# The order of VectorE and ScalarE written by hand through the mixers of a hybrid decoder step, with two open decay levels, sample values loaded ahead of states and the third gates moved up

## The chip, the core and the metric

The kernel runs on one core of one Trainium2 chip. The metric is the device time in microseconds (us) of one execution on that core, the median of several runs. The engines are TensorE (PE, its weight loads PEld), VectorE (DVE), ScalarE (ACT), GpSimd (POOL) and SyncE (SP); in this kernel SyncE issues the DMAs of the weights, and GpSimd those of the samples' states and values.

## The reference, cut

One layer of a decoder with 256 prompt tokens and 8 samples of one new token each (NP = 256, NT = 264 columns of work). The weights are float32.

```python
h = rmsnorm(x, g_pre_mix) * (1.0 + sc1) + sh1       # sc1, sh1, ... = silu(c) @ w_ada: "ada"
z = h @ w_in
(z_uv, hq, hf, hi, hg, gq, gk, gv, gr, glr, z_gate) = split(z)

y_a = spatial_gating(u, layernorm(v), sgu_w_s, sgu_b_s)                # branch A
o_hg, S_hg = gated_linear_recurrence(q_hg, k_hg, hi, log_f, s_hg)      # HGRN, 8 heads
y_b = head_rmsnorm(o_hg, hg_norm_g) * silu(hg)                         # branch B
o_g, S_g = gated_linear_recurrence(q_g, k_g, gv, log_a, s_gla)         # GLA, 4 heads
y_c = head_rmsnorm(o_g, gla_norm_g) * silu(gr)                         # branch C
merged = sum(sigmoid(z_gate)[n] * (branches[n] @ w_branch[n]) for n in range(3))
x = x + gt1 * rmsnorm(merged @ w_out, g_post_mix)
x = x + gt2 * rmsnorm(square(relu(h2 @ w_mlp_up)) @ w_mlp_down, g_post_mlp)
```

A recurrence is `S = f * S + k v^T; o = S^T q` per token. For the prompt it starts from zero; each sample has a state of its own, read from memory, changed by its one token and written back.

## The kernel before, in words

**Granules.** All large products run as a chain of granules of 512 KB of weights, 24 matmuls each: a weight tile is split into a rounded half `whi` (a cast on ScalarE, L109) and the remainder `wlo` (a subtraction on VectorE, L106), and TensorE forms hi x hi, hi x lo and lo x hi (L602 to L604) into an accumulator `mm`. `plan()` lists the granules in order, and SyncE loads them five ahead into four `raw` buffers. The split halves live in six buffers, two to a granule (`SPLIT_AHEAD = 2`), so what is written behind granule p for VectorE or ScalarE stands in program order behind the split of granule p+3.

In order of time the granules are: the input products (0 to 79), the GLA inputs (80 to 113), branch A (114 to 161), the four gate tiles of branch B, `gates_b` (162 to 177), branch B (178 to 225), `gates_c` (226 to 241), branch C (242 to 289), then `w_out` and the MLP, 577 in all. A branch tile is a gate product of four granules and two granules of the branch's own weights; L1296 (branch A) or L1298 with an addition of L103 (B and C) multiplies the two.

**Background.** The mixers run between granules. Generators `mixer_a` (spatial gating), `mixer_r` (one each for HGRN heads 0 to 3 and 4 to 7, and for GLA: groups 0, 1, 2) and `samples_r` (the samples' states of each group) are moved on by `background()` after every granule, at a rate from `RATES`; `READY` stands for the next granule. `mixer_r` forms the gates (`log_sigmoid`, L925 to L931, for group 0 with `lower_bounds`, L906 to L920, ahead, then L961 to L973), opens decay levels whose matmuls (L633) wait in the list `levels`, and ends with the attention between the two halves of 128 tokens: the key product `kd` and the query product `qd` (L1163, L1165, and L100 of VectorE), eight matmuls at L1176, a copy `attx`. `slot()` issues waiting level matmuls and sample reads between granules; the ada products (L342) fill in too.

**Samples.** For each step, `samples_r` loads a state `st` of 256 KB (`fetch`, L1029) and values `vbc` (`values`, L1035), both from GpSimd's queue; ScalarE scales the state (L1055), VectorE adds key times value (L1057), GpSimd stores it (L1058), and when a sample's heads are complete its state is read by L640 into `sm` and added to `os`. At the end stand a square with its sum (L1067), the root by small VectorE instructions (`rstd_small`, L179 to L185) and a scaling (L1069). `FETCHED` is the number of granules between a load and its use. `finish(i)`, at the head of branches B and C, drains what is left of group i, transposes `os` on TensorE (L1256) and copies it (L1257); `parts_c` then multiplies by the gates (L1335) and splits the result for TensorE.

**Who sets the order.** From the first mixer to the last branch (L898 to the exit behind branch 2) TensorE and GpSimd follow the program as written (`manual_schedule`); VectorE's and ScalarE's instructions are placed by the compiler's scheduler.

Of the kernel before, what the change touches and what calls it, by code (L numbers as in the profile page):

```python
# [15 lines left out]
P = 128  # L16
# [31 lines left out]
READY = object()  # L48
SLOT_WAIT = 4
HELD_OWED = 1.0  # L50
LEVELS_HELD = 3
FETCHED = 3
AGE = 2
ADA_LAND = 4

# [2 lines left out]
def hybrid_step_kernel(  # L58
# [438 lines left out]
    rate = [0.0, 0.0]  # L497
# [8 lines left out]
    def plan():  # L506
# [9 lines left out]
        for s in range(4):  # L516
            out += blocks(win, 0, KT, 7168 + s * CW)
        for n in range(N_BRANCH):
            if n:
                g0 = 5120 if n == 1 else 8192  # L520
                for s in range(4):
                    out += blocks(win, 0, KT, g0 + s * CW)
            for m in range(8):
                out += blocks(win, 0, KT, 9232 + n * D + m * CW) + blocks(w_branch[0, n], 0, 8, m * CW)
# [285 lines left out]
    def mixer_a():  # L810
# [71 lines left out]
        for gp in range(4):  # L882
# [12 lines left out]
            )  # L895
            mul(u[:, :, 0:NP], yv[:, :, 0:NP], u[:, :, 0:NP])
            yield
    order = tc.manual_schedule(engines={mybir.EngineType.PE, mybir.EngineType.Pool})  # L898
    order.__enter__()
    gen_a = mixer_a()  # L900
    bg.g.append(gen_a)
# [112 lines left out]
    def samples_r(G):  # L1014
# [12 lines left out]
        def fetch(b, h):  # L1027
            st = tmp([P, nh, dv], "st", ST_BUFS)
            nc.gpsimd.dma_start(st, G.s_in(b, h, nh))  # L1029
            ahead.append((st, now[0]))  # L1030

        def values(b, h):
            v = tmp([P, 4, P], "vbc", VB_BUFS)
            r0 = 4 * nj * b + h * nj
            nc.gpsimd.dma_start(v, vs_d[G.i, r0:r0 + 4, :].partition_broadcast(P))  # L1035
            vals.append((v.rearrange("p (h j) v -> p h (j v)", h=nh), now[0]))
# [8 lines left out]
        for n, (b, h0) in enumerate(steps):  # L1045
            if n + 2 < len(steps):

                yield lambda: len(sts) + sum(len(x[3]) for x in samples) <= ST_BUFS - 3
                fetch(*steps[n + 2])
            if n + 1 < len(steps):  # L1050
                values(*steps[n + 1])
            yield lambda: now[0] >= max(ahead[0][1] + FETCHED, vals[0][1] + FETCHED - 1)
            st, v = ahead.pop(0)[0], vals.pop(0)[0]
            for i in range(nh):
# [18 lines left out]
    def mixer_r(G):  # L1073
# [83 lines left out]
            levels.append((now[0], e, e, m, put))  # L1157

        cv = v4(c, P)
        yield lambda: len(levels) < 2  # L1160
        kd, qd = blk([P, 4, NP]), blk([P, 4, P])
        sub(kd.rearrange("p h (n j) -> p h n j", j=P), cv[:, :, :, 127:128].to_broadcast([P, 4, 2, P]), cv)
        S.activation(qd, c[:, :, P:NP], AF.Exp)  # L1163
# [6 lines left out]
        mul(kd, kd, k[:, :, 0:NP])  # L1170
        yield READY
        yield READY
        attx = blk([P, 4, P])
        ps = sm([P, 4, P])
        for h in range(4):
            T.matmul(ps[:, h, :], kd[:, h, 0:P], qd[:, h, :], start=True, stop=True)  # L1176
# [167 lines left out]
    branch(0, parts_a)  # L1344
    gates_b = gate_tiles(5120)
    rounds.batch = 2
    branch(1, lambda: parts_b(gates_b))
    rate[:] = RATES[2]
    rounds.pace, rounds.batch = 4, 4
    gates_c = gate_tiles(8192)  # L1350
    rate[:] = RATES[3]
    branch(2, lambda: parts_c(gates_c))

    order.__exit__(None, None, None)
# [367 lines left out]
```

## Time and profile before

| what | value |
|---|---|
| median of 3 runs (lowest, highest) | 1940.76 us (1939.07, 1942.31) |
| span of the profiled execution | 1942.9 us (2.1 over that median) |
| TensorE busy / weight loads | 98% / 93% |
| VectorE, ScalarE, GpSimd busy | 61%, 52%, 4% |
| mean granted TensorE clock | 0.994 |
| DMA moved | 442.06 MB, 228 GB/s on the mean |

How to read it. The profile is one execution, and its span runs from the first to the last instruction. TensorE's busy share is the first thing to see: nothing else is near it. A wait is quoted as engine, operation and line, the releaser with its line, then total us, count, longest. A row of a busy-time stretch gives `start:end length`, then busy us and instruction counts of PE, PEld, DVE, ACT and POOL, then the granted clock (1.00 is full), the busy share of the DMA engines and GB/s. In grouped rows `x8` is a count and `busy, mean ns` follow; time in brackets is idle time ahead of an instruction with its releaser. Numbers at the end of tile names (`sm_1835_11308`) are buffer numbers.

### The profile page before, as it was taken

Reading aid. Unit: us, or ns where it says so; the run is one execution under the profiler, and the core shown is the slowest. Engines: PE = TensorE matmul, PEld = TensorE weight load, DVE = VectorE, ACT = ScalarE, POOL = GpSimd, SP = SyncE. Lnnn points to the kernel's source line nnn. Section 1 sums busy time; section 2 is a strip of 40 time slices with the busy share of each in tenths; the row PEclk is TensorE's granted clock in tenths of the full one; section 3 lists DMA queues with packets and bytes.
Section 4 is the critical chain, followed back from the end, with each engine's and each line's share of the span. In section 5 each row is a group of like instructions: output and inputs, shape, how many; then the busy total and the mean of one; then the engine's idle time right before and its main releaser. Section 6 shows DMA issues by size and latency. Waiting matters only on the chain.

```text
span 1942.9 us, 42324 instructions
## 1 busy us (share of the span) xinstructions
PE 1903.4 (98%) x17080; PEld 1812.1 (93%) x17080; DVE 1186.1 (61%) x2103; ACT 1006.5 (52%) x1825; POOL 83.9 (4%) x142
## 2 busy tenths in 40 slices
PE   6999999998999999999999999999999999999998
PEld 5989999988999998999999988999999999999997
DVE  4566667686578695565555666545556555555665
ACT  5444454665666765544444556444444545454444
POOL 1000000001001112200000010000000000000000
PEclk9999999999999999999999999999999999999999
DMA  9897786688588688987777846776566555555552
GB/s 317 299 337 247 249 287 213 214 250 276 175 262 290 214 258 283 306 266 249 253 256 233 300 129 195 229 226 199 178 182 184 179 180 184 177 183 182 179 183 99
DMA packets 339380, 442.06 MB, mean 228 GB/s; under 512 B 14930, under 2 KB 281024, under 8 KB 339184
## 3 DMA queue, kind: packets, MB, share of 16 engines
q1 hardware_dynamic: 329120, 409.62, 65.5%
q0 software_dynamic: 8992, 28.48, 4.6%
q8 instruction: 134, 2.20, 0.5%
q10 hardware_dynamic: 1072, 1.25, 0.2%
q14 instruction: 62, 0.51, 0.1%
HBM read 427.60 MB, written 11.70 MB: 226 GB/s over the span
## 4 chain that ended last, share of the span: by engine, by line
PE 95%; DMA 2%; issue 1%; ACT 1%; DVE 1%; POOL 0%; SPq 0%; ACTq 0%; DVEq 0%; POOLq 0%
PE mm L602 29%; PE mm L603 29%; PE mm L604 28%; PE ada L342 3%; PE ada L274 1%; PE sm L633 1%; PE sm L780 1%; DMA raw<-in_w_in_dram 1%; PE sm L640 0%; DMA b<-in_x_prompt_dram 0%; DMA vbc<-vs_d 0%; DVE wlo L106 0%; DMA b<-in_w_ada_dram 0%; ACT gt L1515 0%; PE sm L1176 0%
## 5 line engine op out<-in xcount | busy, mean ns | idle before, releaser
L602 PE MATMUL mm<-b,whi 128*128 128x264 f32 x4624 | 1326.6, 287 | 7.5 <-ACT b L109 3.5
L603 PE MATMUL mm<-b,whi 128*128 128x264 f32 x4624 | 1317.8, 285 | 0.8 <-DVE b L106 0.8
L604 PE MATMUL mm<-b,wlo 128*128 128x264 f32 x4624 | 1314.5, 284 | 1.4 <-issue 0.7
L106 DVE TENSOR_TENSOR wlo<-raw,whi 128x512 fp32r<-128x512 f32 x1136 | 775.5, 689 | 572.0 <-ACT whi L109 570.0
L109 ACT CAST whi<-raw 128x512 fp32r<-128x512 f32 x1136 | 695.4, 618 | 730.6 <-PE mm L603 654.5
L602 PEld LDWEIGHTS mm<-b,whi 128*128 128x128 f32 x4624 | 872.3, 189 | 49.1 <-issue 26.2
L604 PEld LDWEIGHTS mm<-b,wlo 128*128 128x128 f32 x4624 | 872.5, 189 | 2.2 <-DVE wlo L106 1.1
L603 PEld LDWEIGHTS mm<-b,whi 128*128 128x128 f32 x4624 | 872.2, 189 | 1.4 <-DVE b L106 1.3
L103 DVE TENSOR_TENSOR b<-b,mm 128x528 f32<-128x528 f32 (+1 forms) x137 | 95.7, 700 | 42.7 <-PE mm L604 42.7
L1057 DVE SCALAR_TENSOR_TENSOR st<-vbc,b,st 128x128 f32<-128x128 f32 (+1 forms) x96 | 34.1, 389 | 51.1 <-DMA vbc<-vs_d 44.2
L1055 ACT ACTIVATE st<-st,fs 128x128 f32<-128x128 f32 (+1 forms) x96 | 37.0, 430 | 53.0 <-DMA st<-in_state_hgrn_dram 27.0
L274 PE MATMUL ada<-b,cT 128*32 128x256 f32 (+1 forms) x640 | 35.7, 361 | 7.2 <-DMA b<-in_w_ada_dram 7.0
L342 PE MATMUL ada<-araw,cT 128*32 128x512 f32 x296 | 39.9, 601 | 0.0
L274 PEld LDWEIGHTS ada<-b,cT 128*32 128x32 f32 x640 | 18.2, 115 | 19.7 <-issue 6.4
L100 DVE TENSOR_TENSOR b<-b,b 128x512 f32<-128x512 f32 (+1 forms) x47 | 34.1, 740 | 1.4 <-ACT b L1165 0.9
L1058 POOL DMA_DIRECT2D out_dram<-st x32 | 23.5, 735 | 156.6 <-DVE st L1057 150.8
L342 PE MATMUL ada<-b,cT 128*32 128x512 f32 x216 | 26.2, 593 | 0.0
L106 DVE TENSOR_TENSOR b<-gt,b 128x528 fp32r<-128x528 f32 x32 | 22.7, 708 | 3.9 <-ACT whi L109 0.9
L106 DVE TENSOR_TENSOR b<-b 128x1024 f32<-128x1024 f32 (+1 forms) x24 | 24.3, 1016 | 0.0
L109 ACT CAST whi<-araw 128x512 fp32r<-128x512 f32 x20 | 12.4, 621 | 20.7 <-PE mm L603 19.0
L100 DVE TENSOR_TENSOR gt<-vt 128x528 f32<-128x528 f32 x32 | 22.4, 701 | 0.9 <-ACT vt L1581 0.9
L1587 ACT ACTIVATE b<-vt 128x528 fp32r<-128x528 f32 x32 | 20.7, 647 | 1.0
(339 smaller groups left out, 825.2 us busy)
## 6 DMA issues: line engine op xcount, KB each, us to landing
raw<-in_w_in_dram SPq DMA_DIRECT2D x232, 512.0 KB, 4.7
raw<-in_w_mlp_up_dram SPq DMA_DIRECT2D x128, 512.0 KB, 3.7
raw<-in_w_mlp_down_dram SPq DMA_DIRECT2D x128, 512.0 KB, 3.6
b<-in_w_ada_dram SPq DMA_DIRECT2D x102, 512.0 KB, 6.4
araw<-in_w_ada_dram SPq DMA_DIRECT2D x74, 512.0 KB, 6.0
raw<-in_w_branch_dram SPq DMA_DIRECT2D x48, 512.0 KB, 4.5
raw<-in_w_out_dram SPq DMA_DIRECT2D x32, 512.0 KB, 3.9
b<-in_w_ada_dram SPq DMA_DIRECT2D x32, 256.0 KB, 5.7
```

The source lines that it names most:

```text
L100: V.tensor_tensor(o, a, b, op=ALU.mult)
L103: V.tensor_tensor(o, a, b, op=ALU.add)
L106: V.tensor_tensor(o, a, b, op=ALU.subtract)
L109: S.copy(hi, src)
L274: T.matmul(acc[32 * j:32 * j + 32, 0:n], cT[:, k, :], w[:, n * j:n * j + n], start=k == 0, stop=k == KT - 1)
L342: T.matmul(self.acc[32 * j:32 * j + 32, :], cT[:, k, :], ws[j // 2][:, j % 2 * 512:j % 2 * 512 + 512], start=k == 0, stop=k == KT - 1)
L602: T.matmul(o, a, xh(k + j), start=first and j == 0, stop=False)
L603: T.matmul(o, a, xl(k + j), start=False, stop=False)
L604: T.matmul(o, b, xh(k + j), start=False, stop=last and j == n - 1)
L1055: S.activation(st[:, i, :], st[:, i, :], AF.Copy, scale=fs[:, h0 + i, b:b + 1])
L1057: V.scalar_tensor_tensor(st[:, i, :], v[:, i, :], k[:, h0 + i, NP + b:NP + b + 1], st[:, i, :], ALU.mult, ALU.add)
L1058: nc.gpsimd.dma_start(G.s_out(b, h0, nh), st)
```

## The change

It is one edit to who sets the order, and several to what is written in which place.

- VectorE and ScalarE join TensorE and GpSimd in the written order from L898 on.
- `LEVELS_HELD` goes from 3 to 2, and the last stages of a mixer begin when no level is open (`not levels`) instead of when fewer than two are.
- `FETCHED` goes from 3 to 4, and `samples_r` issues `values` ahead of `fetch`, so ahead of the wait of a state load for its buffer.
- `attx` is written into `qd` instead of a new block.
- The granules of `gates_c` move from behind branch B to right behind `gates_b`: granules 178 to 193, and branch B becomes 194 to 241. The rate 1.25 (`RATES[2]`) isn't used any more: the gates run at 1.6, and 1.0 with `pace` and `batch` of 4 is set ahead of branch C.

```diff
--- before.py
+++ after.py
@@ -48,8 +48,8 @@
 READY = object()
 SLOT_WAIT = 4
 HELD_OWED = 1.0
-LEVELS_HELD = 3
-FETCHED = 3
+LEVELS_HELD = 2
+FETCHED = 4
 AGE = 2
 ADA_LAND = 4
 
@@ -516,8 +516,7 @@
         for s in range(4):
             out += blocks(win, 0, KT, 7168 + s * CW)
         for n in range(N_BRANCH):
-            if n:
-                g0 = 5120 if n == 1 else 8192
+            for g0 in (5120, 8192) if n == 1 else ():
                 for s in range(4):
                     out += blocks(win, 0, KT, g0 + s * CW)
             for m in range(8):
@@ -895,7 +894,7 @@
             )
             mul(u[:, :, 0:NP], yv[:, :, 0:NP], u[:, :, 0:NP])
             yield
-    order = tc.manual_schedule(engines={mybir.EngineType.PE, mybir.EngineType.Pool})
+    order = tc.manual_schedule(engines={mybir.EngineType.PE, mybir.EngineType.Pool, mybir.EngineType.DVE, mybir.EngineType.Activation})
     order.__enter__()
     gen_a = mixer_a()
     bg.g.append(gen_a)
@@ -1046,9 +1045,10 @@
             if n + 2 < len(steps):
 
                 yield lambda: len(sts) + sum(len(x[3]) for x in samples) <= ST_BUFS - 3
-                fetch(*steps[n + 2])
             if n + 1 < len(steps):
                 values(*steps[n + 1])
+            if n + 2 < len(steps):
+                fetch(*steps[n + 2])
             yield lambda: now[0] >= max(ahead[0][1] + FETCHED, vals[0][1] + FETCHED - 1)
             st, v = ahead.pop(0)[0], vals.pop(0)[0]
             for i in range(nh):
@@ -1157,7 +1157,7 @@
             levels.append((now[0], e, e, m, put))
 
         cv = v4(c, P)
-        yield lambda: len(levels) < 2
+        yield lambda: not levels
         kd, qd = blk([P, 4, NP]), blk([P, 4, P])
         sub(kd.rearrange("p h (n j) -> p h n j", j=P), cv[:, :, :, 127:128].to_broadcast([P, 4, 2, P]), cv)
         S.activation(qd, c[:, :, P:NP], AF.Exp)
@@ -1170,7 +1170,7 @@
         mul(kd, kd, k[:, :, 0:NP])
         yield READY
         yield READY
-        attx = blk([P, 4, P])
+        attx = qd
         ps = sm([P, 4, P])
         for h in range(4):
             T.matmul(ps[:, h, :], kd[:, h, 0:P], qd[:, h, :], start=True, stop=True)
@@ -1344,11 +1344,10 @@
     branch(0, parts_a)
     gates_b = gate_tiles(5120)
     rounds.batch = 2
+    gates_c = gate_tiles(8192)
     branch(1, lambda: parts_b(gates_b))
-    rate[:] = RATES[2]
+    rate[:] = RATES[3]
     rounds.pace, rounds.batch = 4, 4
-    gates_c = gate_tiles(8192)
-    rate[:] = RATES[3]
     branch(2, lambda: parts_c(gates_c))
 
     order.__exit__(None, None, None)
```

What this moves is seen in three places. (Lines of the changed kernel between about L520 and L1048 have numbers lower by one: its L601 to L603 are L602 to L604 of before, L639 is L640.) A bare row gives line, operation and `out<-in`; `x4` is four instructions.

**VectorE, the end of HGRN group 0**, where `qd` is multiplied (L100, 128x512) for the matmuls of L1176. Before:

```order
L1057 SCALAR_TENSOR_TENSOR st_981_5855<-vbc_1021_6099,b_838_4812,st_981_5855 128x128 x3
L106 TENSOR_TENSOR wlo_1015_6083<-raw_997_5937,whi_1014_6082 128x512
L1057 SCALAR_TENSOR_TENSOR st_981_5855<-vbc_1021_6099,b_838_4812,st_981_5855 128x128
L1057 SCALAR_TENSOR_TENSOR st_1020_6097<-vbc_1022_6110,b_838_4812,st_1020_6097 128x128 x2
L106 TENSOR_TENSOR wlo_1026_6141<-raw_1002_5982,whi_1025_6140 128x512
L1057 SCALAR_TENSOR_TENSOR st_1020_6097<-vbc_1022_6110,b_838_4812,st_1020_6097 128x128
L1296 SCALAR_TENSOR_TENSOR b_985_5863<-gt_1010_6051,mm_1011_6053 128x528
L106 TENSOR_TENSOR wlo_1028_6145<-raw_1002_5982,whi_1027_6144 128x512
L1057 SCALAR_TENSOR_TENSOR st_1020_6097<-vbc_1022_6110,b_838_4812,st_1020_6097 128x128
L106 TENSOR_TENSOR wlo_1032_6177<-raw_1007_6016,whi_1031_6176 128x512
L100 TENSOR_TENSOR b_1018_6089<-b_1018_6089,b_25_170 128x512
L106 TENSOR_TENSOR wlo_1034_6181<-raw_1007_6016,whi_1033_6180 128x512
```

The product stands behind eight sample updates of L1057, in the same granule as the matmuls that read it. After:

```order
L106 TENSOR_TENSOR wlo_1040_6268<-raw_1025_6134,whi_1039_6267 128x512
L106 TENSOR_TENSOR wlo_1042_6272<-raw_1025_6134,whi_1041_6271 128x512
L106 TENSOR_TENSOR b_1044_6277<-b_27_172 128x1024
L100 TENSOR_TENSOR b_1045_6278<-b_1045_6278,b_25_170 128x512
L100 TENSOR_TENSOR b_1044_6277<-b_1044_6277,b_838_4812 128x1024
L1057 SCALAR_TENSOR_TENSOR st_1017_6085<-vbc_1018_6096,b_838_4812,st_1017_6085 128x128 x4
L106 TENSOR_TENSOR wlo_1048_6320<-raw_1031_6170,whi_1047_6319 128x512
L106 TENSOR_TENSOR wlo_1050_6324<-raw_1031_6170,whi_1049_6323 128x512
L103 TENSOR_TENSOR os0_913_5294<-os0_913_5294,sm_1052_6329 128x128
L106 TENSOR_TENSOR wlo_1058_6371<-raw_1036_6204,whi_1057_6370 128x512
L106 TENSOR_TENSOR wlo_1060_6375<-raw_1036_6204,whi_1059_6374 128x512
```

The product stands ahead of the updates of the second of these states (`st_1020` above is `st_1017` here), and L1176 follows two granules later in TensorE's order.

**TensorE, the last sample reads of GLA (L640) and the transposes of their sum (L1256), at the head of branch C.** Before, in two places, fifteen granules apart:

```order
L604 MATMUL mm_1829_11273<-b_49_302,wlo_1810_11178 128x264
L640 MATMUL sm_1835_11308<-st_1784_11015,b_1474_9011 32x256 x2
L640 MATMUL sm_1835_11308<-st_1786_11024,b_1474_9011 32x256 x2
L602 MATMUL mm_1829_11273<-b_231_1274,whi_1814_11215 128x264
```

```order
L604 MATMUL mm_1906_11749<-b_503_2888,wlo_1910_11779 128x264
L1256 MATMUL sm_1929_11892<-cst_83,os2_1518_9296 128x128
L1256 MATMUL sm_1930_11895<-cst_83,os2_1518_9296 128x128
L602 MATMUL mm_1935_11914<-b_49_302,whi_1912_11808 128x264
```

In the first the states of the last sample are read between the first and the second granule of `gates_c`, and in the second the transposes stand between the last granule of `gates_c` and the first of branch C. After:

```order
L602 MATMUL mm_1906_11785<-b_1551_9569,whi_1894_11720 128x264
L603 MATMUL mm_1906_11785<-b_1550_9568,wlo_1895_11721 128x264
L639 MATMUL sm_1917_11861<-st_1870_11565,b_1511_9285 32x256 x2
L639 MATMUL sm_1917_11861<-st_1872_11574,b_1511_9285 32x256 x2
L1256 MATMUL sm_1923_11885<-cst_83,os2_1559_9609 128x128
L1256 MATMUL sm_1924_11888<-cst_83,os2_1559_9609 128x128
L601 MATMUL mm_1929_11907<-b_49_302,whi_1897_11755 128x264
```

The reads have moved to the transposes, with nothing between them; all stand between the last granule of branch B and the first of branch C. On VectorE the chain between them reads in the changed kernel:

```order
L106 TENSOR_TENSOR wlo_1913_11850<-raw_1896_11724,whi_1912_11849 128x512
L106 TENSOR_TENSOR wlo_1915_11854<-raw_1896_11724,whi_1914_11853 128x512
L1298 SCALAR_TENSOR_TENSOR gt_1905_11783<-gt_1905_11783,mm_1906_11785 128x528
L103 TENSOR_TENSOR b_1258_7581<-b_1258_7581,gt_1905_11783 128x528
L103 TENSOR_TENSOR os2_1559_9609<-os2_1559_9609,sm_1917_11861 128x256
L179 TENSOR_SCALAR sx_1921_11871<-sss_1918_11867 128x1
L181 TENSOR_SCALAR srr_1919_11868<-sx_1921_11871 128x1
L100 TENSOR_TENSOR sa_1922_11872<-srr_1919_11868 128x1
```

The sum `os2` and the root behind it stand after the two operations on branch B's last tile (L1298 and L103), which wait for that last granule; eight more small rows of the root follow.

**ScalarE, the gates of HGRN group 0.** Before:

```order
L925 ACTIVATE b_819_4695<-b_27_172 128x1056
L109 CAST whi_803_4627<-raw_782_4492 128x512
L927 ACT_TABLE_LOAD
L927 ACTIVATE b_819_4695<-b_819_4695 128x1056
L109 CAST whi_805_4631<-raw_782_4492 128x512
L109 CAST whi_808_4662<-raw_789_4534 128x512
L929 ACT_TABLE_LOAD
L929 ACTIVATE b_819_4695<-b_819_4695 128x1056
L109 CAST whi_810_4666<-raw_789_4534 128x512
L802 COPY sqs_814_4674<-sm_813_4672 32x128
L995 COPY b_669_3840<-mm_802_4602 16x264
L109 CAST whi_821_4724<-raw_798_4584 128x512
```

Casts of weights stand between the functions and their table loads. After:

```order
L109 CAST whi_808_4662<-raw_789_4534 128x512
L109 CAST whi_810_4666<-raw_789_4534 128x512
L801 COPY sqs_814_4674<-sm_813_4672 32x128
L908 ACT_TABLE_LOAD
L908 ACTIVATE lb0_815_4677<-lb0_815_4677 128x8
L915 ACT_TABLE_LOAD
L915 ACTIVATE lnlb_3828<-lb3_818_4680 128x8
L919 ACTIVATE lnom_3829<-lb3_818_4680 128x8
L924 ACTIVATE b_819_4695<-b_27_172 128x1056
L926 ACT_TABLE_LOAD
L926 ACTIVATE b_819_4695<-b_819_4695 128x1056
L994 COPY b_669_3840<-mm_802_4602 16x264
L109 CAST whi_821_4724<-raw_798_4584 128x512
```

The functions of `lower_bounds` (L908 to L919) and of `log_sigmoid` (L924, L926) now follow each other, with three table loads between two casts.

## The prediction

> **What bounds the kernel now.** I read the page first, then busy time by stretch for two stages: the mixers with their branches, and the MLP, which the change does not touch.
>
> ```profile
> PE 1903.4 (98%) x17080; PEld 1812.1 (93%) x17080; DVE 1186.1 (61%) x2103; ACT 1006.5 (52%) x1825; POOL 83.9 (4%) x142
> 309.50:1057.90 748.40, 742.23 (x7325) 694.80 (x7324) 487.81 (x905) 426.04 (x819) 72.90 (x111) 1.00 0.78 250
> 1400.00:1700.00 300.00, 300.00 (x2470) 300.00 (x2469) 173.43 (x257) 139.84 (x231) 0.00 (x0) 1.00 0.59 181
> ```
>
> TensorE (first pair of each stretch) is busy 98% of the span and wholly in the MLP: 300 us for 2470 matmuls, 0.1215 us each, so a granule of 24 takes 2.91 us. In the mixer stage 742.2 of 748.4 us are busy. VectorE (487.8) and ScalarE (426.0) have room there, so an order on them can only win what TensorE waits for. Those waits from the mixers to the last branch (line waited for: total us, times, longest):
>
> ```profile
> PE sm L1176 <- DVE b L100: 4.7, 1, 4.7
> PE mm L604 <- issue: 0.7, 1, 0.7
> PE mm L604 <- DVE wlo L106: 0.7, 2, 0.4
> ```
>
> That is 6.1 us in all: the gain is one stall and crumbs. The chain of waits (start, us, what) tells how the stall came about:
>
> ```profile
> 467.17 0.55 POOL vbc L1035
> ...
> 468.46 7.77 DMA vbc<-vs_d
> ...
> 477.73 0.62 DVE b L1296
> ...
> 479.24 0.64 ACT b L1163
> 479.91 0.70 DVE b L100
> 480.66 2.08 PE sm L1176 x8
> 482.74 0.22 PE mm L602
> ...
> 487.04 0.12 PE mm L604
> ```
>
> GpSimd issued a `vbc` load at 467.2, VectorE stood until it landed at 476.2, and the query product that L1176 needs was behind. The stall has a tail: after it a matmul follows the last in 0.22 us, not 0.12. Busy time by stretch gives the granted clock (the figure behind POOL's):
>
> ```profile
> 475.90:480.70 4.80, 0.09 (x2) 0.05 (x1) 4.35 (x10) 1.76 (x3) 0.90 (x2) 0.92 1.04 397
> 480.70:486.80 6.10, 6.10 (x28) 6.10 (x29) 1.19 (x2) 1.20 (x2) 0.00 (x0) 0.50 0.68 221
> ```
>
> It was 0.50 for 6.1 us. In the stretch before it was 0.92 over 4.8 us, which is 0.50 in the last 0.8 us, so the drop came 4.0 us after TensorE stopped and held 6.9 us.
>
> **The change, part by part.** *Removed: the L1176 stall.* The written order puts this query product two granules ahead of L1176 (order rows above); two granules are 5.8 us, against 0.70 us for the product. Gain 4.7 us of wait and half of 6.1 us at half clock, 3.0: **-7.7**.
>
> *Values ahead of states, four granules of lead.* What the loads cost now:
>
> ```profile
> DVE st L1057 <- DMA vbc<-vs_d: 44.2, 14, 6.3
> ACT st L1055 <- DMA st<-in_state_hgrn_dram: 27.0, 7, 7.9
> ACT st L1055 <- DMA st<-in_state_gla_dram: 25.9, 10, 6.9
> POOL st L1029 <- PE sm L640: 130.7, 12, 18.8
> vbc<-vs_d POOLq DMA_DIRECT2D x32, 256.0 KB, 6.7
> ```
>
> GpSimd holds the values' issue behind a state load that waits for a buffer (130.7 us). In the new order the values go first, at least three granules (8.7 us) before use, against a landing of 6.7 us. I take the 44.2 and 52.9 us of waits as mostly gone; only where they reached TensorE do they pay. Of the two small waits (1.4 us) I count half: **-0.7** (bounds 0 and -1.4).
>
> *Added: a wait of TensorE at the head of the last branch.* Four granules of lead also slow the sample states. The last two of the third head group used to be read by L640 fifteen granules before L1256 turns their sum over; now L640 and L1256 stand together behind the last granule of branch B (order rows above). L1256 must wait for the sum, its square, the small root iteration on VectorE and the scaling, and every later granule is queued behind it. In the kernel before, the same chain ran beside matmuls, and L1256 waited for nothing:
>
> ```profile
> 848.59 0.64 PE L640 MATMUL sm<-st,b 128*32 128x256 f32 x8
> 897.20 0.38 PE L1256 MATMUL sm<-cst,os 128*128 128x128 f32 x2
> ```
> ```profile
> 846.33 0.70 DVE L1298 SCALAR_TENSOR_TENSOR gt<-gt,mm 128x528 f32<-128x528 f32 x1
> ...
> 847.55 0.70 DVE L103 TENSOR_TENSOR b<-b,gt 128x528 f32<-128x528 f32 x1
> ...
> 849.85 0.41 DVE L103 TENSOR_TENSOR os<-os,sm 128x256 f32<-128x256 f32 x1
> 850.84 0.15 DVE L179 TENSOR_SCALAR sx<-sss 128x1 f32<-128x1 f32 x1 [0.58 <-ACT vt L1067]
> 851.02 0.15 DVE L181 TENSOR_SCALAR srr<-sx 128x1 int32<-128x1 int32 x1
> ...
> 857.28 0.69 DVE L106 TENSOR_TENSOR wlo<-raw,whi 128x512 fp32r<-128x512 f32 x1 [0.76 <-ACT whi L109]
> ```
> ```profile
> 850.30 0.42 ACT L1067 ACTIVATE vt<-os 128x256 f32<-128x256 f32 x1 [1.10 <-DVE os L103]
> 850.62 0.19 ACT L1067 ACTIVATION_READ_ACCUMULATOR vt<-os 128x1 f32 x1
> ...
> 854.28 0.51 ACT L1069 ACTIVATE os<-os,srr 128x256 f32<-128x256 f32 x1
> ...
> 856.63 0.62 ACT L109 CAST whi<-raw 128x512 fp32r<-128x512 f32 x1 [0.83 <-PE mm L603]
> ```
>
> In the written order VectorE stands at a weight split when TensorE leaves the granule: its buffer comes free only then, the cast takes 0.6 and the subtraction 0.7, with the handovers 1.4 us. Then L1298 and L103 (0.7 each, 0.6 from start to start), the sum 0.4, L1067 0.5 with its read-out, eleven small instructions that start 0.19 apart (2.1), L1069 0.5 and handovers 0.1: 1.4 + 1.2 + 0.4 + 0.5 + 2.1 + 0.5 + 0.1 = 6.2 us. TensorE has L640 for 0.65 of it, so it idles some 5.5 us. With the clock falling 4.0 us into the gap and held 6.9, 5.4 us of matmuls run at half clock: 2.7 lost. **+8.2**, bounds 4.3 (the 1.2 us of L1298 and L103 hidden, no clock loss) and 11.5 (the last `vbc` 3.3 us late, its 10.0 us maximum against 6.7).
>
> [...]
>
> *Everything else in written order.* The same instructions run: VectorE gains one addition, the loads are the same in number, and the table loads keep theirs. What can go wrong is the lead. Six half-granule buffers let a weight split run three granules ahead of its use: with 1.4 us for cast and subtraction, some 5.9 us of cover, plus what other matmuls lie between. The tightest place is the first HGRN gates, where ScalarE now has three table loads in one block between two granules' casts:
>
> ```profile
> L929 ACT ACT_TABLE_LOAD x1 | 1.3, 1283 | 0.0
> L929 ACT ACTIVATE b<-b 128x1056 f32<-128x1056 f32 x1 | 1.1, 1087 | 0.0
> L995 ACT COPY b<-mm 16x264 f32<-16x264 f32 x1 | 0.4, 364 | 0.0
> L802 ACT COPY sqs<-sm 32x128 f32<-32x128 f32 x1 | 0.3, 251 | 0.0
> L1020 ACT ACTIVATE fs<-b 128x32 f32<-128x32 f32 x1 | 0.2, 230 | 2.1 <-DVE b L1099 2.1
> ```
>
> Three loads (3.9), two large functions (2.1), three small ones (0.7, sized as L1020), two copies (0.6) and one exchange with VectorE (0.5 for three small instructions) are 7.8 us. What it may take: cast, block, cast and subtraction must fit three granules (8.7), the ada matmuls among them (1.1) and 0.25 until the first subtracted half is used, or 10.1 - 2.1 = 8.0. So it just fits, and the gate steps behind it alternate the two engines with no lead to spare. I put **+1.0** on this and all other places, bounds 0 and 6.
>
> *Edits at nothing.* Two open levels instead of three, and `not levels` ahead of the last two stages, thin ScalarE's and VectorE's work per granule; the cover is that the third group's mixer still ends fifteen granules ahead of its branch, and without that cover its tail would join the chain above. `attx` in `qd` makes a copy wait for the L1176 matmuls, whose result it reads anyway. Gates C ahead of branch B move sixteen granules past forty-eight without adding any; their weight loads on SyncE's queue move with them, two more go to `araw` and two fewer to blocks, and two blocks stay held. Rate 1.25 becomes 1.6 for these sixteen: more background earlier, in a stretch where the new order has little.
>
> Sum: -7.7 - 0.7 + 8.2 + 1.0 = +0.8 us. Against the profiled span of 1942.9 that is 1943.7; that span lies 2.1 us over the median of the runs, 1940.76, so the forecast for the median is **1941.6 us**. My own range for it is 1937 to 1945.
>
> **Rivals.** *The chain costs TensorE little* (faster). If the last states are added up before the drain, or ScalarE and VectorE stand so far ahead that only L1067 to L1069 (some 3 us) remain, a gap stays under the 4.0 us after which the clock fell. For it: the cover elsewhere is real. Against it: L1298 waits for the very granule behind which L640 stands. It gives -7.7 - 0.7 + 3.0 + 0.5 = -4.9, and with no wait at all -7.9: 1933 to 1936.
>
> *The written order eats the lead at the first gates* (slower). Past 8.0 us the block reaches TensorE, and each gate step behind it, an exchange of cast, subtraction, VectorE and ScalarE of about 4.3 us against a granule of 2.9 to 4.0, adds up to 1.4 us more; three such steps are 3 us, and if one gap is long enough for the clock, 3 us more. It decides when the block takes 0.2 us more than I count. For it: ScalarE has 1.2 us of casts in each granule besides, and there is no scheduler to slip a cast between. Against it: the kernel before ran all but one of the same steps at these places without a wait. Price +3 to +6 on the sum without its 1.0: 1944 to 1947.5, more if a second place (VectorE's normalisation of the first mixer's values) joins.
>
> *The change does not do what it says:* L1057 still waits for its values, and the L1176 stall only moves. Then -7.7 is lost besides: 1949.
>
> **How the numbers follow.** Forecast 0.43; chain cheap 0.22; lead eaten 0.29; stall moved 0.06. About 0.2% (3.9 us) is what a measurement of this kernel can tell from no change: under 1936.9 counts as faster, over 1944.6 as slower. Faster: the cheap chain, and 0.02 of the forecast's edge: 0.24. Slower: lead eaten (0.27 of 0.29), stall moved, and 0.02 of the forecast: 0.35. Within: 0.41. The range takes in the cheap chain down to 1934 and the eaten lead up to 1948.5.
>
> **What would show it.** Right: no wait of L1176 for L100; one wait of L1256 of about 5.5 us near 890 us for ScalarE's `os`, with 0.50 clock behind it; waits of L1057 and L1055 for loads down by most of their 97 us; no wait of L602 to L604 over 1 us between 370 and 420 us. Wrong: L1256 waits under 3 us (the chain), waits for `whi` or `wlo` near 375 to 400 us (the lead), L1057 waiting as before (the loads), or the clock at full rate behind a 5 us gap.

## The result, and the profile after

The changed kernel is **slower**, by 0.85%: 1960.71 us (5 runs, 1959.40 to 1961.62) against 1942.31 us for the kernel before, measured again beside it (5 runs, 1939.07 to 1946.41). The ratio is 1.0085, with a 95% interval from 1.0072 to 1.0097: 18 us lost where +0.8 was forecast.

The page's busy times, then busy time by stretch for the mixers with their branches (the same granules as the stretch shown of before) and for the MLP:

```profile
PE 1907.0 (97%) x17080; PEld 1813.9 (93%) x17080; DVE 1193.7 (61%) x2104; ACT 1006.4 (51%) x1825; POOL 83.7 (4%) x142
```
```profile
307.60:1072.85 765.25, 745.20 (x7321) 696.33 (x7320) 497.18 (x923) 428.99 (x824) 72.73 (x111) 0.99 0.76 245
1400.00:1700.00 300.00, 300.00 (x2469) 300.00 (x2469) 173.80 (x257) 140.14 (x230) 0.00 (x0) 1.00 0.59 181
```

The MLP is as it was. The mixer stage is 765.25 us long instead of 748.40, which is 16.9 us, and so is the difference of the two spans (1959.8 and 1942.9). The part ahead of the stage is 1.9 us shorter and the part behind it as much longer, so the net change is this stage's. The busy times of the four engines hardly moved, so it must be TensorE's waiting and its clock. TensorE's waits in the stage (line waited for: total us, times, longest):

```profile
PE sm L1256 <- ACT os L1069: 6.0, 1, 6.0
PE sm L210 <- DVE vsb L103: 4.6, 1, 4.6
PE sm L779 <- ACT b L1245: 3.2, 2, 1.8
PE sm L632 <- DVE b L100: 3.2, 1, 3.2
PE sm L1243 <- ACT b L1245: 1.1, 1, 1.1
PE sm L632 <- issue: 1.1, 1, 1.1
PE mm L601 <- ACT gt L1289: 0.6, 1, 0.6
PE mm L602 <- issue: 0.2, 1, 0.2
```

L1176 is gone from the list. L1256, the wait that was forecast, heads it, and behind it stand seven smaller ones that weren't. Together 20.0 us, against 6.1 before. The chain that ends in L1256, in order of time (start, us, what; rows between left out):

```profile
903.65 0.56 PE sm L639 x8
904.22 0.69 DVE wlo L106
904.91 0.62 DVE gt L1298
...
909.63 0.52 ACT os L1069
910.19 0.69 PE sm L1256 x2
```

After three of the waits the granted clock also fell to 0.50. Busy time by stretch around them, with the granted clock behind POOL's figure:

```profile
338.40:340.90 2.50, 0.00 (x0) 0.00 (x0) 2.47 (x3) 0.48 (x1) 0.00 (x0) 1.00 0.57 163
340.90:347.70 6.80, 4.78 (x22) 4.79 (x23) 4.81 (x17) 0.62 (x1) 0.00 (x0) 0.50 0.59 171
596.90:600.30 3.40, 1.17 (x76) 0.94 (x80) 3.40 (x7) 0.55 (x2) 0.00 (x0) 1.00 0.69 185
600.30:603.70 3.40, 3.40 (x18) 2.25 (x11) 3.22 (x9) 0.00 (x0) 2.04 (x3) 0.50 0.86 253
603.70:607.10 3.40, 3.40 (x30) 3.40 (x30) 1.58 (x3) 1.24 (x2) 0.00 (x0) 1.00 0.88 288
904.20:907.50 3.30, 0.02 (x4) 0.00 (x0) 2.64 (x6) 0.51 (x2) 0.00 (x0) 1.00 0.81 254
907.50:914.30 6.80, 4.11 (x19) 4.11 (x20) 3.88 (x17) 1.58 (x2) 0.00 (x0) 0.50 0.52 196
```

At 0.50 a matmul follows the last in 0.22 us (from 343.95 us) instead of 0.12 (from 335.99), so about half of the busy time there is lost: 2.4 us behind L210, 1.7 behind L632, 2.1 behind L1256, 6.2 in all, against 3.0 before. Waits 20.0 - 6.1 and clock 6.2 - 3.0 make 17.1 us of the 16.9, so nothing is left over. By places: L1256 with its tail cost 8.1; the other seven cost 14.0 of waits and 4.1 of clock, **18.1 us**; the kernel before had lost 9.1.

The loads did what was forecast: in the tables of VectorE's and ScalarE's waits of the changed kernel the rows for loads of `vbc` and `st`, 97 us before, are gone, and GpSimd's wait ahead of the state loads fell from 130.7 us:

```profile
POOL st L1028 <- PE sm L639: 32.8, 9, 5.9
```

Each of the three kinds of new waits can be seen in a timeline (start, us, instruction, in brackets the idle time before it and its releaser). **A late start**, VectorE ahead of L210: busy time by stretch, of before and of the changed kernel.

```profile
315.00:320.00 5.00, 5.00 (x44) 5.00 (x44) 3.75 (x7) 2.05 (x4) 0.00 (x0) 1.00 0.48 129
320.00:325.00 5.00, 5.00 (x41) 4.83 (x40) 4.79 (x20) 2.48 (x5) 0.00 (x0) 1.00 0.50 156
```
```profile
315.00:320.00 5.00, 5.00 (x45) 5.00 (x44) 2.60 (x5) 2.00 (x4) 0.00 (x0) 1.00 0.40 111
320.00:325.00 5.00, 5.00 (x42) 4.83 (x41) 4.01 (x9) 2.37 (x4) 0.00 (x0) 1.00 0.45 115
330.00:335.00 5.00, 5.00 (x43) 5.00 (x42) 4.76 (x12) 1.99 (x4) 0.00 (x0) 1.00 0.71 228
```

The scheduler had put the first statistics of the normalisation (L831) into VectorE's gaps from 314.8 us on. In written order they stand behind a copy of a small TensorE product (L825) and start at 323.3; VectorE stands idle first and is full afterwards, and the sums for L210, written last, come 4.6 us late. **A foreign wait**, VectorE ahead of L632:

```profile
592.33 1.23 DVE L1057 SCALAR_TENSOR_TENSOR st<-vbc,b,st 128x128 f32<-128x128 f32 x4 [1.51 <-ACT st L1055]
595.97 0.70 DVE L1296 SCALAR_TENSOR_TENSOR b<-gt,mm 128x528 f32<-128x528 f32 x1 [2.41 <-PE sm L632]
596.59 1.28 DVE L106 TENSOR_TENSOR wlo<-raw,whi 128x512 fp32r<-128x512 f32 x2
597.80 1.28 DVE L100 TENSOR_TENSOR b<-b,b 128x512 f32<-128x512 f32 x2
599.00 1.28 DVE L106 TENSOR_TENSOR wlo<-raw,whi 128x512 fp32r<-128x512 f32 x2
```

L1296 writes a new block and reads nothing that L632 makes, yet L632 releases it; so the block must be one that a decay level held until TensorE's L632 had read it. VectorE stands there for 2.4 us, and behind it in the queue is L100, whose product the second half of the same L632 needs. **A queue of casts**, ScalarE ahead of L779:

```profile
525.66 1.56 ACT L1234 ACTIVATE b<-b,rr 128x128 f32<-128x128 f32 x5
527.12 2.17 ACT L109 CAST whi<-raw 128x512 fp32r<-128x512 f32 x4
529.19 1.06 ACT L1245 COPY b<-sm 128x512 f32<-128x512 f32 x2
```

L779 needs a small accumulator that L1245 empties, and four casts for later granules (2.2 us) are written ahead of that copy.

### The profile page after: what moved, and what is told of

It reads as the page before. It is cut to its first block, busy times and chain, and to the rows that moved or that the text cites. A ratio compares the mean times of both kernels' runs of the same rounds, so it can differ in the third digit from the quotient of the medians.

```text
span 1959.8 us, 42413 instructions
## 1 busy us (share of the span) xinstructions
PE 1907.0 (97%) x17080; PEld 1813.9 (93%) x17080; DVE 1193.7 (61%) x2104; ACT 1006.4 (51%) x1825; POOL 83.7 (4%) x142
## 3 DMA queue, kind: packets, MB, share of 16 engines
q10 hardware_dynamic: 1072, 1.25, 0.2%
## 4 chain that ended last, share of the span: by engine, by line
PE 95%; DMA 1%; DVE 1%; ACT 1%; issue 1%; SPq 0%; DVEq 0%; ACTq 0%
PE mm L601 29%; PE mm L602 29%; PE mm L603 28%; PE ada L342 3%; PE ada L274 1%; PE sm L632 1%; PE sm L779 1%; DMA raw<-in_w_in_dram 1%; DMA b<-in_w_ada_dram 1%; ACT whi L109 1%; DVE wlo L106 0%; PE sm L639 0%; DMA b<-in_x_prompt_dram 0%; ACT b L1234 0%; ACT gt L1514 0%
## 5 line engine op out<-in xcount | busy, mean ns | idle before, releaser
L601 PE MATMUL mm<-b,whi 128*128 128x264 f32 x4624 | 1328.9, 287 | 6.7 <-DVE b L103 2.7
L602 PE MATMUL mm<-b,whi 128*128 128x264 f32 x4624 | 1318.0, 285 | 1.5 <-DVE b L106 1.2
L603 PE MATMUL mm<-b,wlo 128*128 128x264 f32 x4624 | 1315.3, 284 | 0.0
L601 PEld LDWEIGHTS mm<-b,whi 128*128 128x128 f32 x4624 | 873.6, 189 | 49.0 <-issue 29.4
L602 PEld LDWEIGHTS mm<-b,whi 128*128 128x128 f32 x4624 | 874.0, 189 | 1.8 <-DVE b L106 1.6
L603 PEld LDWEIGHTS mm<-b,wlo 128*128 128x128 f32 x4624 | 873.5, 189 | 0.3 <-issue 0.3
L103 DVE TENSOR_TENSOR b<-b,mm 128x528 f32<-128x528 f32 (+1 forms) x137 | 95.6, 699 | 43.5 <-PE mm L603 43.5
L342 PE MATMUL ada<-araw,cT 128*32 128x512 f32 x304 | 41.0, 607 | 0.0
L100 DVE TENSOR_TENSOR b<-b,b 128x512 f32<-128x512 f32 (+1 forms) x47 | 33.9, 744 | 10.3 <-ACT b L1121 6.2
L1057 DVE SCALAR_TENSOR_TENSOR st<-vbc,b,st 128x128 f32<-128x128 f32 (+1 forms) x96 | 32.4, 391 | 8.4 <-ACT st L1055 8.4
L1055 ACT ACTIVATE st<-st,fs 128x128 f32<-128x128 f32 (+1 forms) x96 | 34.8, 426 | 0.0
L342 PE MATMUL ada<-b,cT 128*32 128x512 f32 x208 | 26.6, 594 | 0.1
L100 DVE TENSOR_TENSOR gt<-vt 128x528 f32<-128x528 f32 x32 | 22.4, 701 | 0.9 <-ACT vt L1580 0.9
L1120 ACT ACTIVATE b<-b 128x512 f32<-128x512 f32 x12 | 7.7, 643 | 27.7 <-DVE b L106 27.7
```

What stands on the lines that cost most here:

```text
L100: V.tensor_tensor(o, a, b, op=ALU.mult)
L103: V.tensor_tensor(o, a, b, op=ALU.add)
L342: T.matmul(self.acc[32 * j:32 * j + 32, :], cT[:, k, :], ws[j // 2][:, j % 2 * 512:j % 2 * 512 + 512], start=k == 0, stop=k == KT - 1)
L601: T.matmul(o, a, xh(k + j), start=first and j == 0, stop=False)
L602: T.matmul(o, a, xl(k + j), start=False, stop=False)
L603: T.matmul(o, b, xh(k + j), start=False, stop=last and j == n - 1)
```

## The experiments

**Theory A**: the written order on VectorE and ScalarE makes the seven waits, because whatever is written ahead of an operand of TensorE, be it early or idle work, must be done first. **Theory B**: the other edits move TensorE's small matmuls to where operands are late, whoever orders the two engines. All times stand beside the kernel before on the same chip, with ratios to it; its median lay between 1942.1 and 1944.1 us. Differences between two of the changed kernels are taken across chips, so they are good to about 2 us.

### Who orders which engine

Three kernels differ from the changed one in one line only: the scheduler gets both engines back, or ScalarE, or VectorE.

```diff
-    order = tc.manual_schedule(engines={mybir.EngineType.PE, mybir.EngineType.Pool, mybir.EngineType.DVE, mybir.EngineType.Activation})
+    order = tc.manual_schedule(engines={mybir.EngineType.PE, mybir.EngineType.Pool})
```

> The changed kernel with VectorE and ScalarE given back to the scheduler, all other edits kept. Theory A (the written order of the two engines costs the 17 us that the forecast lacked, at the waits of TensorE for L210, L779, L632 and L1243): these waits go; the wait of L1256 for the scaled sum (6.0 us and a tail of about 2) stays, since the last sample reads still stand right ahead of it; about 1942 us, near the kernel before. Theory B (the other edits move TensorE's small matmuls to places where their operands are late, whoever orders the two engines): the waits stay, about 1958 us.

Measured: 1953.6 us (1951.53 to 1957.29), 1.0058 (1.0040 to 1.0075). L210 and L779 wait no more and L632 for L100 only 0.3 us, L1256 still does (5.0 us), so A holds for those. L1243 still waits for L1245 (1.8 us), which A didn't expect. And the time is almost 12 us over the expectation, with new small waits for `wlo` and L1189, and the loads are waited for again. Of its tables of VectorE's and ScalarE's waits:

```profile
DVE st L1057 <- DMA vbc<-vs_d: 43.2, 12, 6.5
```
```profile
ACT st L1055 <- DMA st<-in_state_gla_dram: 45.2, 14, 6.9
ACT st L1055 <- DMA st<-in_state_hgrn_dram: 28.0, 9, 8.0
```

That is as much as before and more, with values ahead of states and four granules of lead in place: the scheduler places L1055 and L1057 earlier than they are written, and the lead is lost. Counted in the casts or subtractions of weights on the same engine, L1055 stands 8.8 granules earlier on the mean than in the changed kernel, and L1057 7.9.

The second has ScalarE scheduled and VectorE written:

```diff
+    order = tc.manual_schedule(engines={mybir.EngineType.PE, mybir.EngineType.Pool, mybir.EngineType.DVE})
```

> The changed kernel with ScalarE given back to the scheduler and VectorE in written order. If each wait belongs to the engine that it names, this keeps L210 (4.6 us and a tail), L632 (3.2 us and a tail) and L1256 (6.0 us and a tail), and loses the waits for ScalarE's copy L1245 (4.3 us) and for L1289 (0.6): about 1955 us. If it takes both engines in written order to make the waits, L210 and L632 go as well: under 1948 us.

Measured: 2001.07 us (1993.56 to 2002.20), 1.0287 (1.0265 to 1.0309). Both expectations missed. VectorE's operations stand in the order written, ScalarE's in the scheduler's: it has L1055 6.4 granules earlier on the mean, stands there 99.4 us for state loads, and the casts that VectorE needs stand behind. TensorE has 41 us of waits, a good many new. That the early state scalings are the whole of this loss is not shown.

The third has VectorE scheduled and ScalarE written:

```diff
+    order = tc.manual_schedule(engines={mybir.EngineType.PE, mybir.EngineType.Pool, mybir.EngineType.Activation})
```

> The changed kernel with VectorE given back to the scheduler and ScalarE in written order. If each wait belongs to the engine that it names: no wait at L210 or L632, the waits for L1245 stay (some 4 us), L1256 stays (6 us and a tail): about 1948 us. If ScalarE's written order holds up the casts, and through them VectorE: 1955 us or more, with L210 waiting still.

Measured: 1947.31 us (10 runs, 1945.41 to 1949.54), 1.0021 (1.0012 to 1.0031), as theory A had it. TensorE's waits in the mixers:

```profile
PE sm L1256 <- ACT os L1069: 5.0, 1, 5.0
PE sm L779 <- ACT b L1245: 2.4, 2, 1.8
PE sm L632 <- issue: 1.5, 1, 1.5
PE sm L1243 <- ACT b L1245: 0.9, 1, 0.9
PE ada L342 <- issue: 0.5, 1, 0.5
```

No L210, no L100, and no row for a load of `vbc` or `st` in the waits of VectorE and ScalarE; L1055 and L1057 stand where they are written. So ScalarE's written order gains some 6 us over the scheduler (1953.6 to 1947.3) and ends the waits for loads; VectorE's on top of it **loses 13.4** (1947.3 to 1960.7). These two figures don't hold apart from each other: with ScalarE scheduled, VectorE's written order loses 47 (1953.6 to 2001.1).

### The order without the other edits

The kernel before with the written order, and of the other edits only those on blocks.

```diff
-LEVELS_HELD = 3
+LEVELS_HELD = 2
...
+    order = tc.manual_schedule(engines={mybir.EngineType.PE, mybir.EngineType.Pool, mybir.EngineType.DVE, mybir.EngineType.Activation})
...
+        yield lambda: not levels
...
+        attx = qd
```

> The kernel before with the written order on all four engines, and of the other edits only those on the blocks (two open levels, the last stages at no open level, the copy into qd); three granules of lead, states ahead of values, and the third gates behind branch B as before. Theory A: waits at L210 (about 4.6 us, with a half-clock tail of 2.4), and some of those of L779, L633 and L1243; no wait at L1256 (four granules between the last sample read and the transposes); 1950 us or a little more. Theory B: about 1942 us.

Measured: 1960.81 us (1960.36 to 1961.55), 1.0093 (1.0078 to 1.0108). L210 (4.6) and L633 for L100 (3.9) are there, which is A. But it is 10 us over the expectation, with two waits at the head of branch B that the changed kernel doesn't have there; none was expected at L1256:

```profile
PE sm L1243 <- ACT b L1234: 5.8, 2, 5.1
PE sm L210 <- DVE vsb L103: 4.6, 1, 4.6
PE sm L633 <- DVE b L100: 3.9, 2, 3.2
PE sm L1256 <- ACT os L1069: 3.6, 1, 3.6
```

In TensorE's order L1176 of HGRN group 1 stands behind granule 175 here (166 before), and branch B begins at 178, so the end of that mixer is drained in one piece there. It is the edits on open levels that put it there, not the written order: L1176 of group 1 stands behind granule 175 also in the first of the three runs above, where the scheduler has both engines, and TensorE follows the program in all of them. Waits for loads are 1.4 us in this run (VectorE's for `vbc`, none of ScalarE's for `st`), with states ahead of values and three granules of lead as in the kernel before: it is the written order that ends them. To see whether moving the third gates up is what hides it, that edit alone (with its rates) was undone, in the changed kernel and then in the fastest one (below).

```diff
-            for g0 in (5120, 8192) if n == 1 else ():
+            for g0 in ((5120,), (8192,))[n - 1] if n else ():
...
-    gates_c = gate_tiles(8192)
     branch(1, lambda: parts_b(gates_b))
-    rate[:] = RATES[3]
+    rate[:] = RATES[2]
     rounds.pace, rounds.batch = 4, 4
+    gates_c = gate_tiles(8192)
+    rate[:] = RATES[3]
```

> The changed kernel with the third gates back behind branch B, at the rate of before. If moving them up hides the end of the second mixer, that mixer's last stages (L1243 and the chain to L1256, some 9 us of waits and a half-clock tail of 3 in the run with the order and only the edits on blocks) come back at the head of branch B: about 1970 us. If the place of the gates has no cost, as the forecast had it, 1960.7 us.

> The fastest kernel so far (1935.6 us: ScalarE alone in written order, three granules of lead, the granule ahead of L779) with the third gates back behind branch B. If the place of the gates is what hides the second mixer's end, 8 to 12 us more, about 1945 us. If the scheduler on VectorE hides that chain by itself, as in the kernel before, 1936 us.

Measured: 1970.34 us (1969.00 to 1972.61) and 1947.47 us (10 runs, 1947.18 to 1948.44). The two waits are back in both; of the second kernel (its L1244 and L1257 are L1243 and L1256):

```profile
PE sm L1244 <- ACT b L1235: 5.8, 2, 5.1
PE sm L1257 <- ACT os L1069: 3.6, 1, 3.6
```

Sixteen granules of gates between the second mixer and its branch are worth 9.6 us in the changed kernel and 11.8 in the other (7.9 and 11.1 when each is taken against the kernel before on its own chip).

### Each wait by itself

*L1256.* The changed kernel with one line undone.

```diff
-FETCHED = 4
+FETCHED = 3
```

> The changed kernel with three granules of lead instead of four; the last sample reads then stand eight granules ahead of L1256. If the 6.0 us wait of L1256 is the sample chain alone, it goes with its tail: 8 us less, about 1952.6 us, and L210 waits 4.6 us as before. If the shorter lead brings the waits for loads back to TensorE, the gain is given back: about 1958 to 1961 us, with a wait at L1176 or L639.

Measured: 1953.86 us (1952.64 to 1957.64), 6.9 less. No row for L1256, and 0.6 us of VectorE for a state load; new are 2.1 us for `whi` and `wlo` in branch C. The wait was the sample chain, and three granules of lead are enough for the loads where ScalarE's order is written.

*L210, first try.* The samples' sums written ahead of the prompt's normalisation.

```diff
+        vs = tmp([P, 8, NS], "vsa", 1)
+        w8 = tmp([P, 8, NS], "vsb", 1)
+        r8 = tmp([P, NS], "vsr", 1)
+        for i in range(2):
+            V.tensor_copy(vs[:, 4 * i:4 * i + 4, :], vF[i][:, :, NP:NT])
+        V.tensor_copy(w8, vs)
+        fold(w8, 8)
         for v in vtk:
...
-        fold(w8, 8)
         yield READY
```

> The changed kernel with the copies and additions for the samples of the first mixer (vsa, vsb) written ahead of the normalisation of the prompt's two halves, where the scheduler had put them in the kernel before. If their place in VectorE's order is the cause of the wait at L210, 4.6 us and the tail of 2.4 go: 7 us less, about 1953.7 us. If VectorE is short of time in this stretch as a whole, the wait comes back at the second L210 or at L886: 1958 us or more.

Measured: 1960.29 us (1958.33 to 1960.58). The first L210 is served and the second waits:

```profile
PE sm L210 <- DVE vsb L103: 3.7, 1, 3.7
```

So the place of these few instructions wasn't it; what is behind them was late too. *Second try*: the statistics written earlier, into the time in which VectorE was idle.

```diff
+        def stats(t, v):
+            st = tmp([P, 2, 6], "bst", 1)
...
+            stat.append((ag, rs))
+
+        stats(0, vtk[0])
+        yield
         wsT = blk([P, 8, P])
...
+        stats(1, vtk[1])
+        yield
         yield READY
         ps = sm()
```

> The changed kernel with the statistics of the first mixer's normalisation (two rows of L830, the aggregation and the root, about 3.9 us for each half) written earlier: those of the first half right behind the transposes, those of the second ahead of the small product of L824, where VectorE had some 4.7 us idle between 312 and 323 us. If the wait of L210 comes of that idle time in front of a backlog, it goes: 4.6 us and the tail of 2.4, about 1953.7 us. If these rows then hold up the weight splits behind them, waits for whi or wlo near 320 to 330 us take its place: 1958 us or more.

Measured: 1955.97 us (1954.11 to 1956.62), 4.7 less. L210 waits 1.6 instead of 4.6 us and its clock stays at 1.00, but a wait at L602 grew from 0.2 to 0.9 us. The late start was the cause of two thirds of the wait; what makes the last 1.6 us is open.

*L779.* One granule between a mixer's last transposes and the next one's first.

```diff
         vb = [blk([P, 2, 512]) for _ in range(nj)]
+        yield READY
         yield from rows_of(G.v, lambda t, g: vb[g // 2][:, t, (g % 2) * CW:(g % 2 + 1) * CW])
```

> The changed kernel with one granule put between a mixer's last transposes (L1243) and the next mixer's first (L779), so that ScalarE has 2.9 us more for the copies L1245 which empty the small accumulators. If the two waits of L779 (1.4 and 1.8 us) are ScalarE's lateness behind four casts, both go: 3.2 us less, about 1957.5 us. If ScalarE is behind for longer than a granule, they stay; and since all later background moves by a granule, the wait of L632 (3.2 us and a tail of 1.7) may go or grow, so 1955 to 1962 us.

Measured: 1956.48 us (1955.83 to 1958.80), 4.2 less. The waits of L779 for L1245 are gone; 0.7 us for another copy (L788) is left. All of TensorE's waits in the mixers fell by 2.4 us in this trace. The changed kernel also has the clock at 0.50 from 105.4 to 108.8 us, ahead of the mixers, 1.7 us of loss. The mean clock of its profiled execution was 0.992 and is 0.993 here, with about 17.1 us at 0.50 from 300 us to 1140 us in both, so that stretch may be missing here; nothing in the edit reaches it, so a part of the 4.2 us may not be the edit's.

*L632.* L1296 of the even tiles of branch A, which takes the block, written two granules later.

```diff
             if n == 0 and m % 2 == 0:
-                mg[m // 2] = blk()
+                def first(m=m, gt=gt, pr=pr):
+                    mg[m // 2] = blk()
+                    V.scalar_tensor_tensor(pair(mg[m // 2], 0), gt, 1.0, pr, ALU.add, ALU.mult)
+
+                later.append((now[0] + 1, first))
+                continue
```

> The changed kernel with the multiplication L1296 of branch A's even tiles, which takes a new block, written two granules later, so that it stands behind the level product (L100) that TensorE's L632 reads. If the 3.2 us wait of L632 comes of VectorE standing at L1296 for a block that the first half of the same L632 has to free, it goes with its tail of 1.7: about 1956 us. If VectorE is late for another reason, L632 waits as before and the time is 1960 us or, with the accumulator held longer, more.

Measured: 1958.90 us (1958.64 to 1959.92), 1.8 less, which is within what the chips differ by; the trace is clearer. The wait of L632 for L100 fell from 3.2 to 0.3 us and its clock stays at 1.00, so L1296 ahead of L100 was the cause. The gain is less than that sum of 4.6: issue waits at L632 and L342 grew by 1.0 us, and the half-clock time of L210 fell almost wholly on busy time in this run (3.2 us lost instead of 2.4).

### Together

All four repairs in the changed kernel (the four edits above):

> The changed kernel, both engines in written order, with the four repairs together: three granules of lead, statistics first, the granule ahead of L779, L1296 two granules later. If the losses are four separate places, the gains add: 1960.7 - 6.9 - 4.7 - 4.2 - 4.9 = 1940 us. If a written order only moves its waits about, 1948 us or more.

Measured: 1943.37 us (11 runs, 1940.31 to 1945.74), 1.0000 (0.9991 to 1.0009). The losses are separate and the repairs add: 6.9, 4.7, 4.2 and 1.8 us one by one are 17.6, together they gain 17.3. That leads back to the time of before: 9 us of small waits stay, none with a clock behind it. Next, only the edit on the loads in the kernel before, with the scheduler on both engines:

```diff
-                fetch(*steps[n + 2])
             if n + 1 < len(steps):
                 values(*steps[n + 1])
+            if n + 2 < len(steps):
+                fetch(*steps[n + 2])
```

> The kernel before with one edit of the change: values issued ahead of the state load and of its wait for a buffer; the scheduler keeps VectorE and ScalarE. If the late values were the cause of the stall at L1176, it goes with its half-clock tail: 4.7 + 3.0 = 7.7 us less, about 1934.6 us. If VectorE's place for the query product behind the sample updates is the cause, and the values are waited for as before, 1942 us.

Measured: 1948.22 us (11 runs, 1944.34 to 1951.21), 1.0024 (1.0013 to 1.0035). L1176 (L1177 here) still waits 2.3 us, VectorE still stands 32.3 us for `vbc`, and there are new waits. Both expectations missed; with the scheduler on both engines the place of one load moves more than that load. And last, VectorE left to the scheduler, ScalarE written, three granules of lead and the granule ahead of L779:

> The changed kernel with VectorE given back to the scheduler, ScalarE in written order, three granules of lead, and the granule between L1243 and L779. From the run with ScalarE alone in written order (1947.3): minus the 6.9 us that three granules of lead gained with both engines, minus some 2 for the two waits of L779: about 1938 us, under the kernel before. If the gains overlap with what the scheduler does anyway: 1942 us or more.

Measured: **1935.63 us** (5 runs, 1934.64 to 1936.92), 0.9961 (0.9949 to 0.9974): faster than both kernels. Its mixer stage and TensorE's waits in it (L1416 and L1534 belong to what follows):

```profile
307.10:1047.70 740.60, 738.67 (x7322) 691.81 (x7321) 493.30 (x916) 431.24 (x824) 72.99 (x111) 1.00 0.79 253
```
```profile
PE sm L632 <- issue: 1.1, 1, 1.1
...
PE mm L603 <- DVE wlo L106: 0.5, 1, 0.5
PE sm L779 <- DVE b L788: 0.3, 1, 0.3
```

Of 740.60 us TensorE is idle for 1.9, and the clock never falls.

## Why the prediction was wrong, point by point

- **The bound** held: all of the change in time is TensorE's waiting and its clock in the mixer stage.
- **L1176, -7.7**: right in size, the wait and its tail are gone. The reason given, the written order, isn't needed: the wait is gone too where the scheduler has both engines and the other edits stay. The run with values ahead alone shows that the load order by itself doesn't do it; which edit does is open.
- **Loads, -0.7**: the waits went as forecast, and the two crumbs with them. The reason was wrong: values ahead and four granules of lead left 116 us of waits for loads where the scheduler had both engines and 99.4 where it had ScalarE. With ScalarE's order written there were none, or 0.6 us with three granules, and with both orders written and neither load edit 1.4 us.
- **L1256, +8.2**: right. The chain is as it was added up, 6.0 us of wait against 5.5, with 2.1 us of clock against 2.7, and undoing the lead took 6.9 us off. The rival of a cheap chain is out.
- **"Everything else in written order", +1.0 with bounds 0 and 6**, is the step that failed: 18.1 us by the trace. With it the sum comes out: -7.7 - 1.4 + 8.1 + 18.1 = 17.1 us, against 16.9. The step put the whole risk on the lead of the weight splits, and on the first HGRN gates above all. There nothing happened:

```profile
370.00:420.00 50.00, 50.00 (x456) 45.94 (x456) 31.66 (x58) 37.27 (x60) 4.14 (x7) 1.00 0.71 226
```

  TensorE is busy for all of the 50 us. What the step didn't do was to follow each small matmul of TensorE (L210, L632, L779, L1243) to its operand and look what stands ahead of that in the two queues. The order shows it: the samples' sums for L210 stand 80 rows later on VectorE than before (they ran at 274 us then, at 342 now). The slower rival blamed the written order too, but by weight splits that come late, and TensorE's table has no row for `whi` or `wlo`. Only its last words, VectorE's normalisation of the first mixer's values, name a place that did cost: that work stands ahead of the sums for L210. Its times are also up to 0.9 us too high for its price: 3 to 6 us on a sum of -0.2 is 1943.6 to 1946.6. And the 1934 and 1948.5 at the end of its chances lie outside the range of 1937 to 1945.
- **Edits at nothing**: the gates' place was costed at nothing for the cover of the third mixer. It was worth 8 to 10 us, for the second mixer, whose end the edits on open levels, costed at nothing as well, had moved from granule 166 to 175 (L1176). One hid the other, so in the changed kernel the two together cost nothing that the trace shows, which is luck: the prediction looked at the third mixer's cover alone. L1296 waited for a block; whether the edits on blocks made that wait was not tried.
- **The clock** was taken to fall 4.0 us after TensorE stops. It fell 2.5 us after (L210), 3.3 after (L1256), and behind a wait of only 3.2 us (L632), when TensorE already ran again. Behind L1256 it held for 6.8 us, as the sum had it (6.9); the loss was 2.1 us and not 2.7, because TensorE was idle for 2.7 us of that time, not for the 1.5 that the sum had.

## What to carry to other kernels

A written order fixes what an engine does while it would otherwise be idle, and puts every operand behind whatever is written ahead of it: before writing one, follow each small matmul of the bound engine to its operand and list what stands in front, waits for buffers included. Do it one engine at a time, and measure; here ScalarE's gained 6 us and VectorE's on top of it lost 13, VectorE's alone lost 47, and the pair looked like one change. A written order of the engine that uses loads can do more for them than the order and the lead of the loads. A move that seems to have no cost can be what hides a chain that another part of the change has made late.

## What the runs showed of the hardware

In the changed kernel's mixers the granted clock fell to 0.50 at 340.9, 600.3 and 907.5 us, and it was 1.00 again 6.8, 3.4 and 6.8 us later. In the kernel before it was 0.50 from 480.0 to 486.8 us. TensorE started again 2.0 us after the fall at L210 and 2.7 us after it at L1256, so that much of the 6.8 us passed without work; at L632 it had started again 1.2 us ahead of the fall and was busy for all of the 3.4 us. The tails therefore don't follow the waits: 2.4 us lost behind a wait of 4.6 (L210), 1.7 behind 3.2 (L632), 2.1 behind 6.0 (L1256).

In the 3.4 us ahead of each fall TensorE had been idle for 2.5 us (L210), 2.2 (L632), 3.3 (L1256) and, in the kernel before, all 3.4 (L1176). The 1.17 us of work between 596.9 and 600.3 us did not prevent the fall. How much idle time it takes is not shown: of two other stretches of 3.4 us in the changed kernel, the clock stayed at 1.00 behind the one from 689.1 us, with 1.8 us idle, and fell to 0.50 behind the one from 1941.8 us, behind the mixers, with 1.65 us idle.
